# Hybrid encoder layer on one core: first-layer sums from GpSimd to VectorE, weight splits five products ahead, other load order in the drain and the mLSTM prelude

## Chip, core and metric

The kernel runs on one core of a Trainium2 chip, as one program. The metric is the device time of an execution in microseconds (us). TensorE (PE) does the matrix products, VectorE (DVE) and ScalarE (ACT) elementwise work, GpSimd (POOL) elementwise work and small steps, and SyncE (SP) only issues DMAs: its queue is in order, so a DMA that waits holds up those behind it.

## What is computed

```python
h = rms_norm(x, g_mix_norm)
z = h @ w_in                           # q, k, v, gate, i/f gates | latents, rotary key
y_a = mlstm_group(...)                 # bidirectional chunkwise mLSTM, 16 chunks of 128
y_b = mla_group(...)                   # 4 heads, softmax over all 2048 keys
x = x + concat(y_a, y_b) @ w_out       # out-projection, 1024 x 1024
h = rms_norm(x, g_ffn_norm)
x = x + square(relu(h @ w_ff1)) @ w_ff2  # 1024 -> 4096 -> 1024
```

x is 2048 x 1024, float32. Every product is done with both operands split into a high and a low part (`split`: ACT casts the high part at L48, DVE subtracts it at L49 to get the low part), as three matmuls per pair (L63 to L65).

## The kernel before

The projections at the start are placed by a scheduler and are the same in both kernels. All that follows is issued in an order written out by hand, engine by engine in program order:

- **Attention with mLSTM** (about 460 to 1160 us of the trace): 32 blocks of 256 queries, eight steps each. Each step issues scores (L1010 to L1014), their scaling by DVE with a running maximum (`p<-ps`, L1015), transposes of probabilities (`ptp`, L1045), their split (`pth`, `ptl`) and products with V (`pv`). A generator, advanced once a step, issues the mLSTM besides: first its gate arithmetic, called the prelude here (L556 to L660), then its chunks. In the prelude the decay table is stored (`d_dec`, L617) and loaded back as `decb` (L619). Each attention block also stores its inverse row sums (`d_rd`, L1031) and loads them back broadcast as `rb` (L1036), which scales the block's output `y` (L1062).
- **Drain** (1150 to 1190 us): the last blocks' products, while `OutProj.weights` loads the 4 MB of `w_out` in 256-KB halves into eight stage tiles (L1198) and splits them (`woh`, `wol`), one pair of halves a step; a half beyond the eighth takes the stage tile of a half just split. The tokens' tiles `y` and `x` go into a ring of eight tiles (`r`).
- **Out-projection** (1190 to 1376 us): 16 token tiles, `residual` (L1280), `normalise` (L1304) and `combine_x` (L1322), which forms sums of the normalised input for the first layer.
- **First feed-forward layer** (1376.75 to 2050 us): a two-level Strassen-like scheme. 32 passes `n` (16 groups of 256 columns for each half of the tokens) of seven products, twelve 128x512 matmuls each. For each product a 128x512 weight block, an original one or a sum of `w1_combine` (L1371), is split some products ahead (`w1_split`, tiles `r`, DVE `r L49`). Each product's PSUM result `pu` is added by DVE into accumulators `e` (L1470), and in four of the seven products ACT then does relu (L1473) and square (L1474). Sums of the results are formed by `u_combine` (L1507) and stored for the second layer. From n = 1 a generator `tokens` normalises and transposes the other half's eight token tiles between products (L1300 to L1322); from n = 14 `exchange` loads and splits that half's operands (L1404, L1405).
- **Second feed-forward layer** (2050 us to the end).

Of the kernel before, what the change touches and what calls it, by code (L numbers as in the profile page):

```python
# [18 lines left out]
P = 128  # L19
# [525 lines left out]
def mlstm_prelude(c, psM):  # L545
# [4 lines left out]
    with ExitStack() as st:  # L550
# [26 lines left out]
        nc.vector.reciprocal(wi, w)  # L577
        nc.vector.tensor_tensor(d, d, wi, op=ALU.mult)
        yield
        nc.vector.tensor_tensor(ln, ln, d, op=ALU.add)  # L580
        nc.vector.scalar_tensor_tensor(f, f, 0.0, ln, op0=ALU.min, op1=ALU.subtract)
        b, u, cu, gs = sb("b"), sb("u"), sb("cu"), sb("gs", (P, 2))
# [32 lines left out]
        nc.scalar.activation(it, M, AF.Exp, scale=-1.0, bias=mp)  # L615
        nc.scalar.activation(gd, gd, AF.Exp, scale=-1.0)
        nc.sync.dma_start(c.d_dec, dec)  # L617
        for par in range(2):
            nc.sync.dma_start(  # L619
                c.dec[par * 64:(par + 1) * 64],  # L620
                c.d_dec.rearrange("(a p c) o -> p o a c", p=2, c=NT)[par].to_broadcast((64, 4, NT)))
        yield
        x1, x2 = sb("x1", (P, 3, P)), sb("x2", (P, 2, P))
        p2 = bank()[:, 0:256].rearrange("p (a t) -> p a t", a=2)
# [6 lines left out]
            nc.tensor.transpose(p1[:, j, :], t, c.ident)  # L631
        yield
        nc.vector.tensor_copy(x1, p1)
        yield
        p4 = bank()[0:H, 0:256].rearrange("p (a t) -> p a t", a=2)
        for j in range(2):
# [32 lines left out]
def mlstm_steps(c, pool, ps, ld):  # L669
# [171 lines left out]

    kws, outs = {}, {}
    first = NT - 1
    for t in range(NT + 2):
        ch = first - t
        if ch >= 1:
            kws[ch] = weigh(1, NT - 1 - ch, ld[ch][1])
        if 1 <= ch + 1 <= first:
            v1 = ld.pop(ch + 1)[0]
            outs[ch + 1] = outer(kws.pop(ch + 1), v1)  # L850
        yield
        if 1 <= ch + 2 <= first:
# [3 lines left out]
        if t in (8, 10, 12, NT + 1):  # L856
            loads[{8: 0, 10: 1, 12: 2}.get(t, 3)](0)
        yield
    for d in range(2):
# [317 lines left out]
class OutProj:  # L1177
# [12 lines left out]
    def weights(self):  # L1190

        nc, c = self.c.nc, self.c
        raws = []

        def load(n):
            k, j = divmod(n, 2)
            raw = self.stage.tile([P, 512], F32, name="raw")
            nc.sync.dma_start(raw, c.w_out[k * P:(k + 1) * P, j * 512:(j + 1) * 512])  # L1198
            raws.append(raw)

        for n in range(8):
            load(n)
        yield
        self.yp = Ring(self.ent_ring(c.tc.tile_pool(name="ring", bufs=4, side="right", reuse_waits="tile")))
        self.wp = self.ent_w(c.tc.tile_pool(name="o_w", bufs=1, side="right", reuse_waits="tile"))
        yield
        for k in range(KD):
            if k in (1, 3):
                self.load_y(k // 2)
            elif k > 5:  # L1210
                self.load_x(k - 6)
            wh = self.wp.tile([P, D], F32R, name=f"woh{k}")
            wl = self.wp.tile([P, D], F32R, name=f"wol{k}")
            for j in range(2):
                cs = slice(j * 512, (j + 1) * 512)
                split(nc, wh[:, cs], wl[:, cs], raws.pop(0), eng=nc.gpsimd if j else None)
                if 2 * k + j + 8 < 2 * KD:
                    load(2 * k + j + 8)
            self.wo.append((wh, wl))
            yield  # L1220

# [96 lines left out]
def combine_x(c, b, t):  # L1318

    b11, b21, b12, b22 = b  # L1320
    for o, x, y in ((t[0], b12, b11), (t[1], b22, t[0]), (t[2], b22, b12), (t[3], b21, t[1])):
        c.nc.gpsimd.tensor_tensor(o, x, y, op=ALU.subtract)  # L1322


def store_x(c, g, i, b, t):
# [5 lines left out]
class FeedForward:  # L1331
# [35 lines left out]
    def w1_combine(self, n, name):  # L1367

        a, b, f = {"S1": ("A21", "A22", ALU.add), "S2": ("S1", "A11", ALU.subtract),
                   "S3": ("A11", "A21", ALU.subtract), "S4": ("A12", "S2", ALU.subtract)}[name]  # L1370
        self.c.nc.gpsimd.tensor_tensor(self.w1_part(n, name), self.w1_part(n, a), self.w1_part(n, b), op=f)  # L1371

    def w1_split(self, n, op):
        if (n, op) < (0, 2):
# [5 lines left out]
        self.w1[n, op] = wh, wl  # L1380

    def h_load(self, g, op, k):
        nc = self.c.nc
# [131 lines left out]
    def tokens(self):  # L1515

        c, nc = self.c, self.c.nc
        for i in range(4):
            b = []
            for q in range(2):  # L1520
                t = 8 + 4 * q + i
                for j in range(2):
                    x = self.stage.tile([P, 512], F32, name="raw")
                    nc.sync.dma_start(x, c.d_x1[t * P:(t + 1) * P, j * 512:(j + 1) * 512])
                    b.append(x)
            junk = self.stage.tile([P, 512], F32, name="raw")
# [11 lines left out]
            combine_x(c, b, tt)  # L1538
            for _ in range(4):
                yield  # L1540
            store_x(c, 1, i, b, tt)
            for _ in range(4):
                yield

    def layer1(self, extra):
        N = 2 * self.NU
        prev = None
        for n in range(N):
            g, f = divmod(n, self.NU)
            if n == 1:  # L1550
                extra = self.tokens()
            elif n == self.NU - 2:
                for _ in extra:
                    pass
                extra = self.exchange()
            for p in range(7):
                self.product(n, p)
                m, q = divmod(7 * n + p + 3, 7)
                if m < N:
                    self.w1_split(m, q)  # L1560
                self.flush()
                if n > 0:
                    if p == 1:
                        self.u_combine(n - 1, "S1")
                        self.u_combine(n - 1, "S2")
                    elif p == 2:
                        self.u_combine(n - 1, "S3")
                    elif p == 3:
                        self.u_combine(n - 1, "S4")
                if prev:  # L1570
                    self.evacuate(*prev)
                prev = n, p, self.ps
                if p == 0:
                    self.w1_combine(n, "S4")
                elif p == 1 and n + 1 < N:
                    self.w1_combine(n + 1, "S1")
                    self.w1_combine(n + 1, "S2")
                elif p == 3:
                    if n + 2 < N:
                        self.load_w1(n + 2)  # L1580
                    if n + 1 < N:
                        self.w1_combine(n + 1, "S3")
# [151 lines left out]
def out_and_ffn(c):  # L1734
    tc = c.tc
    with ExitStack() as s_stage:
        with ExitStack() as s_e:
# [10 lines left out]
            with ExitStack() as s_y:  # L1748
# [14 lines left out]
                for s in range(NT - 2):  # L1763
# [10 lines left out]
                    if s < 8:  # L1774
                        o.normalise(s)
                    if s % 2 == 0 and 2 <= s <= 8:
                        combine_x(c, *pair)
# [9 lines left out]
                    if s == 12:  # L1787
                        ff.load_w1(0)
                        ff.load_w1(1)
                    elif s == 13:  # L1790
                        for name in ("S1", "S2", "S3"):
                            ff.w1_combine(0, name)
                        ff.w1_split(0, 0)
# [3 lines left out]
                ff.w1_split(0, 1)  # L1797
                for _ in range(3):
                    pieces_on(4)
                for i in range(2):  # L1800
                    o.residual(NT - 2 + i, po[i])
            with ExitStack() as s_ps:
                ff.open1(s_f1.enter_context, s_ps.enter_context)
                ff.w1_split(0, 2)
                prev = ff.layer1(ff.h_pieces(0, pieces))
                s_f1.close()
                s_h1.close()
# [45 lines left out]
```

## Time and profile before

| | |
|---|---|
| median of 3 runs | 2668.52 us (2662.75 to 2672.58) |
| profiled execution | 2668.72 us, span 2666.9 us |
| PE busy | 2594.1 us, 97% |
| VectorE busy | 1615.9 us, 61% |
| ScalarE busy | 1193.9 us, 45% |
| GpSimd busy | 826.3 us, 31% |

The span is from the first to the last recorded instruction; the 1.8 us between it and the execution's time are start and end. Times in the rows are from the span's start. An engine's busy share is over the whole span, so it says little of a single stage.

### The profile page before, as it was taken

How to read it: one execution, taken by the hardware profiler on the slowest of the kernel's cores; microseconds unless marked ns; L12 is line 12 of the kernel's file. 1: busy time of each engine (PE TensorE's matmuls, PEld its weight loads, DVE VectorE, ACT ScalarE, POOL GpSimd, SP SyncE). 2: the span in 40 equal slices, each digit the busy share in tenths (PEclk: the TensorE clock that was granted, in tenths of full speed). 3: DMA queues.
4: the chain of work that ended last, by engine and by line, in shares of the span. 5: the costliest groups of instructions: out<-in, count | busy, mean ns of one | idle time of the engine just before them, and what ended most of it. 6: DMA issues, size and time to landing. Idle time of an engine off the chain costs nothing. (4 is left out here: it accounts for less than half of the span.)

```text
span 2666.9 us, 37134 instructions
## 1 busy us (share of the span) xinstructions
PE 2594.1 (97%) x13227; PEld 2180.9 (82%) x13227; DVE 1615.9 (61%) x2914; ACT 1193.9 (45%) x2457; POOL 826.3 (31%) x730
## 2 busy tenths in 40 slices
PE   8999999899999999989999999989999999999999
PEld 6888887788888888878887777668887888888887
DVE  5585475666666666654356666666666477666443
ACT  6455443446656566542134444544444333332332
POOL 1211210123224232212116666555655133233000
PEclk9999999999999999999999999999999999999999
DMA  4344244245464565446664555834445844444552
GB/s 154 122 131 153 95 134 135 70 118 125 92 117 108 92 115 101 68 127 190 210 208 137 169 196 170 256 135 141 146 154 173 316 150 142 143 143 153 206 174 103
DMA packets 298870, 391.58 MB, mean 147 GB/s; under 512 B 33281, under 2 KB 187196, under 8 KB 298684
## 3 DMA queue, kind: packets, MB, share of 16 engines
q1 hardware_dynamic: 296380, 385.01, 49.0%
q10 hardware_dynamic: 2304, 4.20, 0.4%
q8 instruction: 104, 1.70, 0.3%
q14 instruction: 82, 0.67, 0.1%
HBM read 256.94 MB, written 132.17 MB: 146 GB/s over the span
## 5 line engine op out<-in xcount | busy, mean ns | idle before, releaser
L63 PE MATMUL pd<-w2h,uh 128*128 128x512 f32 x896 | 349.3, 390 | 1.3 <-ACT w2h L48 1.3
L64 PE MATMUL pd<-w2l,uh 128*128 128x512 f32 x896 | 349.4, 390 | 0.4 <-DVE w2l L49 0.4
L65 PE MATMUL pd<-w2h,ul 128*128 128x512 f32 x896 | 349.3, 390 | 0.0
L49 DVE TENSOR_TENSOR ul<-ur,uh 128x1024 fp32r<-128x1024 f32 x110 | 146.9, 1336 | 253.7 <-ACT uh L48 253.5
L49 DVE TENSOR_TENSOR ptl<-ptp,pth 128x512 fp32r<-128x512 f32 x256 | 176.7, 690 | 193.8 <-ACT pth L48 193.7
L48 ACT CAST uh<-ur 128x1024 fp32r<-128x1024 f32 x110 | 116.0, 1054 | 396.3 <-PE pd L64 378.4
L49 DVE TENSOR_TENSOR r<-w1raw,r 128x512 fp32r<-128x512 f32 x160 | 187.6, 1173 | 140.8 <-ACT r L48 140.8
L48 ACT CAST pth<-ptp 128x512 fp32r<-128x512 f32 x256 | 149.2, 583 | 253.7 <-PE ptp L1045 252.3
L1473 ACT ACTIVATE e<-e 128x512 f32<-128x512 f32 x128 | 80.9, 632 | 346.8 <-DVE e L1470 346.8
L1507 POOL TENSOR_TENSOR e<-e 128x512 f32<-128x512 f32 x128 | 183.4, 1443 | 120.8 <-ACT e L1474 118.2
L1015 DVE TENSOR_SCALAR_CACHE_REDUCE p<-ps 128x512 f32<-128x512 f32 x256 | 175.1, 684 | 45.4 <-PE ps L1014 44.1
L63 PEld LDWEIGHTS pd<-w2h,uh 128*128 128x128 f32 x896 | 168.6, 188 | 36.8 <-ACT w2h L48 1.8
L64 PEld LDWEIGHTS pd<-w2l,uh 128*128 128x128 f32 x896 | 168.6, 188 | 36.1 <-DVE w2l L49 1.1
L65 PEld LDWEIGHTS pd<-w2h,ul 128*128 128x128 f32 x896 | 168.5, 188 | 35.0
L63 PE MATMUL pv<-pth,vh 128*128 128x256 f32 x512 | 146.3, 286 | 15.1 <-DVE y L1062 7.7
L1629 POOL TENSOR_TENSOR r<-wr,r 128x512 f32<-128x512 f32 x48 | 87.0, 1813 | 223.3 <-DMA wr<-in_w 141.0
L1045 PE MATMUL ptp<-ident,p 128*128 128x128 f32 x1024 | 154.2, 274 | 0.0
L63 PE MATMUL pz<-wh,hh 128*128 128x512 f32 (+1 forms) x384 | 150.3, 393 | 3.1 <-ACT hh L48 3.1
L65 PE MATMUL pz<-wh,hl 128*128 128x512 f32 (+1 forms) x384 | 150.7, 393 | 0.0
L1470 DVE TENSOR_TENSOR e<-pu,e 128x512 f32<-128x512 f32 x224 | 149.6, 680 | 1.4 <-POOL e L1507 1.2
L64 PE MATMUL pz<-wl,hh 128*128 128x512 f32 (+1 forms) x384 | 150.3, 391 | 0.0
L64 PE MATMUL pv<-ptl,vh 128*128 128x256 f32 x512 | 146.2, 285 | 1.1 <-DVE ptl L49 0.9
(392 smaller groups left out, 6832.4 us busy)
## 6 DMA issues: line engine op xcount, KB each, us to landing
d_u<-e SPq DMA_DIRECT2D x224, 256.0 KB
ur<-d_u SPq DMA_DIRECT2D x110, 512.0 KB
w1raw<-in_w SPq DMA_DIRECT2D x64, 512.0 KB
wr<-in_w SPq DMA_DIRECT2D x96, 256.0 KB
raw<-in_w_in SPq DMA_DIRECT2D x48, 256.0 KB
xt<-in_x SPq DMA_DIRECT2D x16, 512.0 KB
mb<-d_M SPq DMA_DIRECT2D x32, 256.0 KB
r<-in_x SPq DMA_DIRECT2D x16, 512.0 KB
```

The source lines that it names most:

```text
L48: nc.scalar.copy(hi, src)
L49: (eng or nc.vector).tensor_tensor(lo, src, hi.bitcast(F32), op=ALU.subtract)
L63: nc.tensor.matmul(out, ah, bh, start=first, stop=False)
L64: nc.tensor.matmul(out, ah, bl, start=False, stop=False)
L65: nc.tensor.matmul(out, al, bh, start=False, stop=last)
L1015: nc.vector.tensor_scalar(probs[b, a][:, j, :], o, SCALE, None, op0=ALU.mult, op1=ALU.max, accum_out=maxes[b, a][:, j:j + 1])
L1045: nc.tensor.transpose(pt[:, k, :], p[:, j, k * P:(k + 1) * P], c.ident)
L1470: nc.vector.tensor_tensor(out, o, t, op=ALU.add)
L1473: nc.scalar.activation(t, t, AF.Relu)
L1507: self.c.nc.gpsimd.tensor_tensor(o, a, b, op=f)
L1629: nc.gpsimd.tensor_tensor(R, wr, R, op=ALU.subtract)
```

## The change

- **Sums.** `combine_x`, `w1_combine` and `u_combine` are issued on VectorE and no longer on GpSimd: 16 sums in the out-projection, and in the first layer 16 of `combine_x`, 128 of `w1_combine` and 128 of `u_combine`. They are issued one per step, behind the step's evacuation. `u_combine` has its four at products 1 to 4 (before: 1, 1, 2, 3).
- **Splits.** A generator `weights1` issues the first layer's splits, sums and loads in their order. From n = 1 to n = 12 it is five products ahead, elsewhere three (before: three everywhere); it takes up to two splits in a step until it is there. The split tiles alternate between both halves of the ring (eight tiles) up to n = 12.
- **Drain.** The rows of w_out for k = 4 to 7 are loaded at once, as four 512-KB transfers into four ring tiles, ahead of the first split; the `y` and `x` loads stand a step or more elsewhere.
- **mLSTM prelude.** One more step stands between the exchange of the gates and their sums (L580 to L583). The two `decb` loads are issued three steps later. The backward chunk loop has one step less.

```diff
@@ mLSTM prelude
         nc.vector.tensor_tensor(d, d, wi, op=ALU.mult)
         yield
+        yield
         nc.vector.tensor_tensor(ln, ln, d, op=ALU.add)
@@
         nc.sync.dma_start(c.d_dec, dec)
-        for par in range(2):
-            nc.sync.dma_start(
-                c.dec[par * 64:(par + 1) * 64],
-                c.d_dec.rearrange("(a p c) o -> p o a c", p=2, c=NT)[par].to_broadcast((64, 4, NT)))
         yield
...
         nc.vector.tensor_copy(x1, p1)
+        for par in range(2):
+            nc.sync.dma_start(
+                c.dec[par * 64:(par + 1) * 64],
+                c.d_dec.rearrange("(a p c) o -> p o a c", p=2, c=NT)[par].to_broadcast((64, 4, NT)))
@@
-    for t in range(NT + 2):
+    for t in range(NT + 1):
@@ OutProj.weights
         self.wp = self.ent_w(c.tc.tile_pool(name="o_w", bufs=1, side="right", reuse_waits="tile"))
+        for k in range(4, KD):
+            if k == 6:
+                self.load_y(0)
+                yield
+            raw = self.yp.tile([P, D], F32)
+            nc.sync.dma_start(raw, c.w_out[k * P:(k + 1) * P, :])
+            raws += [raw[:, 0:512], raw[:, 512:]]
         yield
         for k in range(KD):
...
                 split(nc, wh[:, cs], wl[:, cs], raws.pop(0), eng=nc.gpsimd if j else None)
-                if 2 * k + j + 8 < 2 * KD:
-                    load(2 * k + j + 8)
@@ combine_x, w1_combine, u_combine
-        c.nc.gpsimd.tensor_tensor(o, x, y, op=ALU.subtract)
+        c.nc.vector.tensor_tensor(o, x, y, op=ALU.subtract)
+        yield
...
-        self.c.nc.gpsimd.tensor_tensor(o, a, b, op=f)
+        self.c.nc.vector.tensor_tensor(o, a, b, op=f)
@@ layer1
                 self.product(n, p)
-                m, q = divmod(7 * n + p + 3, 7)
-                if m < N:
-                    self.w1_split(m, q)
+                ahead = 7 * n + p + 1 + (5 if 0 < n < self.NU - 3 else 3)
+                todo = min(2, ahead - self.nsplit)
+                for i in range(todo):
+                    next(self.wsteps, None)
+                    if i + 1 < todo:
+                        next(self.wsteps, None)
                 self.flush()
...
                 prev = n, p, self.ps
...
+                if todo > 0:
+                    next(self.wsteps, None)
+                if n > 0 and 1 <= p <= 4:
+                    self.u_combine(n - 1, f"S{p}")
                 next(extra, None)
```

SP in the prelude, behind the first store of an inverse row sum that stands there (`d_rd`; `dec` tiles are the decay table, `raw<-d_kn` and `d_kr` the keys of the next head). Before:

```order
L1031 DMA d_rd<-rd_5115 128x2x1
L617 DMA d_dec<-dec 128x1
L619 DMA decb<-d_dec 64x4x16 x2
L1036 DMA rb<-d_rd 128x256
L953 DMA raw<-d_kn 128x512
L956 DMA raw<-d_kr 64x512 x2
L1031 DMA d_rd<-rd_5267 128x2x1
```

and now:

```order
L1032 DMA d_rd<-rd_5115 128x2x1
L1037 DMA rb<-d_rd 128x256
L618 DMA d_dec<-dec 128x1
L954 DMA raw<-d_kn 128x512
L957 DMA raw<-d_kr 64x512 x2
L632 DMA decb<-d_dec 64x4x16 x2
L1032 DMA d_rd<-rd_5255 128x2x1
```

The load of `rb` moved ahead of the table's store and load; the table's load moved behind the keys.

SP in the drain, behind the last mLSTM store (`d_ya`; `r` are ring tiles, the loads of `in_w_out` the out-projection's weights). Before:

```order
L838 DMA d_ya<-sgt 128x512
L1198 DMA raw<-in_w_out 128x512 x2
L1235 DMA r_13345<-d_ya 128x512
L1236 DMA r_13345<-d_yb 128x4x128
L1198 DMA raw<-in_w_out 128x512 x2
L1031 DMA d_rd<-rd_13179 128x2x1
L1198 DMA raw<-in_w_out 128x512 x2
L1065 DMA d_yb<-y 128x256
L1235 DMA r_13401<-d_ya 128x512
L1236 DMA r_13401<-d_yb 128x4x128
L1198 DMA raw<-in_w_out 128x512 x2
L1036 DMA rb<-d_rd 128x256
```

and now:

```order
L839 DMA d_ya<-sgt 128x512
L1212 DMA r_13307<-in_w_out 128x1024
L1212 DMA r_13309<-in_w_out 128x1024
L1240 DMA r_13311<-d_ya 128x512
L1241 DMA r_13311<-d_yb 128x4x128
L1212 DMA r_13333<-in_w_out 128x1024
L1212 DMA r_13335<-in_w_out 128x1024
L1032 DMA d_rd<-rd_13182 128x2x1
L1240 DMA r_13373<-d_ya 128x512
L1241 DMA r_13373<-d_yb 128x4x128
L1066 DMA d_yb<-y 128x256
L1037 DMA rb<-d_rd 128x256
```

All weights stand ahead of `d_rd` now; between the last `d_yb` and `rb` two loads of `in_x` are left out of the second fence.

DVE in the first layer, in a pass without token work (`r` split tiles, `w1raw` loaded weights, `sw` weight sums). Before:

```order
L49 TENSOR_TENSOR r_16132<-w1raw_15939,r_16132 128x512
L1470 TENSOR_TENSOR e<-pu,e 128x512
L49 TENSOR_TENSOR r_16151<-sw,r_16151 128x512
L1470 TENSOR_TENSOR e<-pu,e 128x512 x2
L49 TENSOR_TENSOR r_16178<-w1raw_15941,r_16178 128x512
L1470 TENSOR_TENSOR e<-pu,e 128x512
```

and now:

```order
L49 TENSOR_TENSOR r_16241<-w1raw_16061,r_16241 128x512
L1500 TENSOR_TENSOR e<-pu,e 128x512
L1377 TENSOR_TENSOR w1raw_16061<-w1raw_16061 128x4x128
L1537 TENSOR_TENSOR e<-e 128x512
L49 TENSOR_TENSOR r_16270<-sw,r_16270 128x512
L1500 TENSOR_TENSOR e<-pu,e 128x512
L1537 TENSOR_TENSOR e<-e 128x512
L49 TENSOR_TENSOR r_16291<-w1raw_16063,r_16291 128x512
L1500 TENSOR_TENSOR e<-pu,e 128x512
L1377 TENSOR_TENSOR w1raw_16063<-w1raw_16063,sw 128x4x128
L1537 TENSOR_TENSOR e<-e 128x512
```

One or two sums (L1377, L1537) now stand behind an addition of a product's result (L1500), where before the next split stood.

## Rows read from the trace of the kernel before

**Rows 1.** Windows: length, busy us of PE, PEld, DVE, ACT, POOL, PEclk, DMA share, GB/s.
```profile
462.00:523.00 61.00, 49.50 (x266) 41.16 (x265) 36.76 (x103) 27.34 (x40) 12.54 (x16) 0.94 0.22 61
523.00:1150.00 627.00, 624.41 (x4246) 555.94 (x4245) 406.27 (x1059) 370.97 (x812) 175.83 (x184) 1.00 0.53 105
1150.00:1190.00 40.00, 29.00 (x181) 25.54 (x180) 23.84 (x52) 24.48 (x50) 12.55 (x10) 0.87 0.57 142
1190.00:1376.00 186.00, 186.00 (x881) 155.12 (x880) 78.42 (x114) 40.72 (x87) 34.50 (x43) 1.00 0.66 207
1396.08:1678.12 282.04, 267.81 (x1157) 214.95 (x1156) 177.82 (x214) 129.69 (x240) 181.35 (x144) 0.98 0.52 169
1678.12:1759.02 80.90, 67.19 (x253) 49.38 (x252) 57.37 (x62) 41.67 (x66) 39.97 (x25) 0.94 0.66 217
1759.02:2010.27 251.25, 251.25 (x1093) 205.24 (x1092) 161.96 (x180) 118.28 (x207) 152.50 (x104) 1.00 0.43 144
```

**Rows 2.** Waits of PE, 462 to 523: total, times, longest (us).
```profile
PE pv L63 <- DVE y L1062: 5.6, 1, 5.6
PE ps L1010 <- DVE p L1015: 4.1, 1, 4.1
```

**Rows 3.** Timeline of DVE, 475 to 517: start, us, instruction, [idle before <-releaser].
```profile
477.15 0.58 DVE L580 TENSOR_TENSOR ln<-ln,d 128x128 f32<-128x128 f32 x1 [1.61 <-ACT ln L574]
...
480.44 0.66 DVE L1015 TENSOR_SCALAR_CACHE_REDUCE p<-ps 128x512 f32<-128x512 f32 x1
...
516.00 0.42 DVE L1062 TENSOR_TENSOR y<-pv,rb 128x256 f32<-128x256 f32 x1 [6.43 <-DMA rb<-d_rd]
```

**Rows 4.** Timeline of SP's DMA issues, 487 to 508.
```profile
487.93 0.37 SPq L1031 DMA_DIRECT2D d_rd<-rd  x1
496.10 0.34 SPq L617 DMA_DIRECT2D d_dec<-dec  x1
505.28 1.27 SPq L619 DMA_DIRECT2D decb<-d_dec  x2
506.65 0.55 SPq L1036 DMA_DIRECT2D rb<-d_rd  x1
```

**Rows 5.** Timeline of ACT in the drain.
```profile
1182.38 1.27 ACT L48 CAST woh<-raw 128x512 fp32r<-128x512 f32 x2 [2.50 <-DMA raw<-in_w_out]
1183.55 0.58 ACT L48 CAST pth<-ptp 128x512 fp32r<-128x512 f32 x1
```

**Rows 6.** Timeline of SP's DMA issues in the drain.
```profile
1167.14 0.38 SPq L1031 DMA_DIRECT2D d_rd<-rd  x1
...
1177.17 0.33 SPq L1036 DMA_DIRECT2D rb<-d_rd  x1
```

**Rows 7.** Timeline of PE at the end of the drain.
```profile
1184.18 0.58 PE L63 MATMUL pv<-pth,vh 128*128 128x256 f32 x1 [6.22 <-ACT pth L48]
...
1188.78 0.48 PE L63 MATMUL po<-woh,r 128*128 128x512 f32 x1
```

**Rows 8.** Timeline of all engines, 969 to 976: a load of `rb` and its use.
```profile
969.31 0.33 SPq L1036 DMA_DIRECT2D rb<-d_rd  x1
...
974.93 0.41 DVE L1062 TENSOR_TENSOR y<-pv,rb 128x256 f32<-128x256 f32 x1
```

**Rows 9.** Waits of VectorE, 1396 to 1759.
```profile
DVE r L49 <- ACT r L48: 82.9, 50, 1.9
DVE raw L1304 <- POOL nr L59: 25.2, 8, 4.2
```

**Rows 10.** Timeline of DVE in pass 24 of the first layer.
```profile
1899.76 0.69 DVE L49 TENSOR_TENSOR r<-w1raw,r 128x512 fp32r<-128x512 f32 x1 [1.87 <-ACT r L48]
1900.37 0.68 DVE L1470 TENSOR_TENSOR e<-pu,e 128x512 f32<-128x512 f32 x1
1902.92 1.38 DVE L49 TENSOR_TENSOR r<-sw,r 128x512 fp32r<-128x512 f32 x1 [1.87 <-ACT r L48]
...
1919.27 0.69 DVE L49 TENSOR_TENSOR r<-w1raw,r 128x512 fp32r<-128x512 f32 x1 [1.87 <-ACT r L48]
```

More of the change, by code (lines that the diff above doesn't have):

```diff
@@ L855, in mlstm_steps @@
             ld[ch - 3] = mlstm_v(c, ch - 3), mlstm_k(c, ch - 3)
-        if t in (8, 10, 12, NT + 1):
+        if t in (8, 10, 12, NT):
             loads[{8: 0, 10: 1, 12: 2}.get(t, 3)](0)
@@ L1199, in load @@
             raws.append(raw)
-        for n in range(8):
+        for n in range(KD):
             load(n)
@@ L1205, in weights @@
         self.wp = self.ent_w(c.tc.tile_pool(name="o_w", bufs=1, side="right", reuse_waits="tile"))
+        for k in range(4, KD):
[5 more added lines that the diff above has]
+            raws += [raw[:, 0:512], raw[:, 512:]]
         yield
         for k in range(KD):
[L1208 to L1213, printed above, removed]
+            if k == 1:
+                self.load_y(1)
+            elif k in (3, 4):
+                self.load_x(k - 3)
+            wh, wl = (self.wp.tile([P, D], F32R, name=f"wo{part}{k}") for part in "hl")
             for j in range(2):
@@ L1370, in w1_combine @@
                    "S3": ("A11", "A21", ALU.subtract), "S4": ("A12", "S2", ALU.subtract)}[name]
-        self.c.nc.gpsimd.tensor_tensor(self.w1_part(n, name), self.w1_part(n, a), self.w1_part(n, b), op=f)
+        self.c.nc.vector.tensor_tensor(self.w1_part(n, name), self.w1_part(n, a), self.w1_part(n, b), op=f)
     def w1_split(self, n, op):
-        if (n, op) < (0, 2):
+        if n < self.NU - 3:
             w = self.ring.tile([P, 2, 4, P], F32R)
@@ L1380, in w1_split, with weights1 @@
         self.w1[n, op] = wh, wl
+    def weights1(self):
+        N = 2 * self.NU
+        self.nsplit = 0
+        self.w1_combine(0, "S1")
+        self.w1_combine(0, "S2")
+        for n in range(N):
+            for q in range(7):
+                self.w1_split(n, q)
+                self.nsplit += 1
+                yield
+                if q == 0:
+                    self.w1_combine(n, "S3")
+                elif q == 2:
+                    self.w1_combine(n, "S4")
+                elif q == 5 and n + 1 < N:
+                    self.w1_combine(n + 1, "S1")
+                elif q == 6:
+                    if n + 2 < N:
+                        self.load_w1(n + 2)
+                    if n + 1 < N:
+                        self.w1_combine(n + 1, "S2")
+                yield
     def h_load(self, g, op, k):
@@ L1537, in tokens @@
             tt.append(junk)
-            combine_x(c, b, tt)
-            for _ in range(4):
-                yield
+            yield from combine_x(c, b, tt)
             store_x(c, 1, i, b, tt)
@@ L1557, in layer1 @@
                 self.product(n, p)
-                m, q = divmod(7 * n + p + 3, 7)
-                if m < N:
-                    self.w1_split(m, q)
-                self.flush()
[L1562 to L1569, printed above, removed]
+                ahead = 7 * n + p + 1 + (5 if 0 < n < self.NU - 3 else 3)
[4 more added lines that the diff above has]
+                        next(self.wsteps, None)
+                self.flush()
                 if prev:
@@ L1572, in layer1 @@
                 prev = n, p, self.ps
[L1573 to L1582, printed above, removed]
+                if todo > 0:
+                    next(self.wsteps, None)
+                if n > 0 and 1 <= p <= 4:
+                    self.u_combine(n - 1, f"S{p}")
                 next(extra, None)
@@ L1776, in out_and_ffn @@
                     if s % 2 == 0 and 2 <= s <= 8:
-                        combine_x(c, *pair)
+                        for _ in combine_x(c, *pair):
+                            pass
                     o.load_x(s + 2)
@@ L1790, in out_and_ffn @@
                     elif s == 13:
-                        for name in ("S1", "S2", "S3"):
-                            ff.w1_combine(0, name)
-                        ff.w1_split(0, 0)
+                        ff.wsteps = ff.weights1()
+                        next(ff.wsteps)
                 po = o.project(NT - 2, NT - 1)
@@ L1796, in out_and_ffn @@
                 ff.open_h1(s_h1.enter_context)
-                ff.w1_split(0, 1)
+                next(ff.wsteps)
+                next(ff.wsteps)
                 for _ in range(3):
@@ L1803, in out_and_ffn @@
                 ff.open1(s_f1.enter_context, s_ps.enter_context)
-                ff.w1_split(0, 2)
+                for _ in range(3):
+                    next(ff.wsteps)
                 prev = ff.layer1(ff.h_pieces(0, pieces))
```

## The prediction

> **What bounds the kernel now.** I read PE's share first: it is busy 97% of the span (the table above), so apart from fewer matmuls only some 73 us of idle PE can be won, and what it loses to a lower clock. The windows by stage tell where that is [rows 1]: 11.5 us in the prelude (462 to 523), 2.6 in the 627 us of attention behind it, 11.0 in the drain, nothing in the out-projection and nothing in passes 17 to 29 of the first layer, where 13 passes take 251.25 us, 19.33 each. At that pace passes 1 to 13 would take 251.3 and took 282.04; passes 14 to 16 would take 58.0 and took 80.90. So 30.7 and 22.9 us lie there, and the change touches just these places.
>
> What bounds passes 1 to 16 is not seen in PE's row but in VectorE's waits [rows 9]: it waits for ACT (82.9 us) and for GpSimd's small steps (25.2 us), never for PE. DVE and ACT are one chain, late throughout, and PE waits for its split weights. The timeline shows a link [rows 10]: DVE splits (1899.76), adds a product's result 0.61 later, then stands 1.87 us while ACT does relu, square and the next cast; the next split starts 3.16 us after the first. The reader is to see two things: this idle time, four times a pass, and that the subtraction of 0.69 us becomes 1.38 in the next row, which I read as GpSimd's sums beside it. Four such steps, two of split and addition (1.22) and one of a split alone (0.61) are 15.7 us; the same row of the next pass comes 19.51 later (1919.27). The 3.8 us between I take for that contention. With 19.51 against PE's 19.33, the chain is as slow as PE even without the tokens' work.
>
> **First layer.** Taken from GpSimd and added on DVE: eight 128x512 sums a pass. No row shows such a sum on DVE; the nearest is the addition, pitch 0.61 (1899.76 to 1900.37); the other end is 1.38, a subtraction beside GpSimd. I take 0.61, since GpSimd then has no sums. In the order now shown the sums stand behind the addition, so in a relu step up to two (1.22) hide in the 1.87 us of idle; in the other steps they lengthen the chain. Five products ahead, products 1, 2 and 4 are the others, with two sums each: 15.7 + 6 x 0.61 = 19.3 a pass. Three ahead it is five sums: 18.7.
> Passes 1 to 12: (19.3 - 19.5) x 12 = -2. Two more splits taken at n = 1: 2 x 0.61, +1.3. Pass 13 leaves two out and is three ahead after them: -0.8 - 1.3 = -2. Passes 14 to 16, three ahead: -0.8 x 3 = -2.5. `combine_x` adds 16 sums on DVE, half of them hidden: +4.9, against contention of as many sums now, which I take as 5.5: -0.6. Pass 0 ends with the chain less late, since its sums no longer run beside the splits of h: -2, an estimate. Together about **-8**. The 25.2 us of waits in the normalisation stay, as its small steps remain on GpSimd.
> The lead of five products I cost at nothing in itself. It lets PE run on while the chain catches up; where the chain is late on average, it only moves the wait. Two products more are 2 x 2.76 = 5.5 us of PE once, and n = 13 falls back to three. Without lateness on average it would be worth much; that is the first rival.
> In passes 17 to 31, PE is full at 19.33 and the chain at 18.7 is now the faster: no change.
> Bounds: with the six unhidden sums at 1.38 a pass is 24.0, +54 in passes 1 to 12; as GpSimd is no partner any more I go a good third of that way, to +20. The other end is the first rival's -47. The out-projection's 16 sums lie under a PE that is full for 186 us with DVE busy 78 [rows 1]: nothing; without that cover, 16 x 0.61 = 10.
>
> **Prelude.** Two stalls. At 516.00 DVE waits 6.43 us for `rb` and PE 5.6 behind it [rows 2, 3]. `rb` was issued at 506.65 because it stood behind `decb`, which waited from 496.10 to 505.28 for the store of `d_dec` [rows 4]. Now `rb` stands right behind its own store, `d_rd`, of 487.93; the nearest price of that wait is the drain's, 1167.14 to 1177.17, 10.0 us [rows 6]. So it is issued at about 498, lands as long after as now (516.0 - 506.7 = 9.4) at 507.3, and is wanted at 509.6: 2.3 us to spare, all 5.6 gone. Queued behind the waiting `rb` are `d_dec` (two us later) and the keys of the next head; behind `decb`, which may wait until 507, only the next `d_rd` at about 509. With the stall goes a clock dip: the granted clock was 0.94 over 61 us, 3.7 us of full-speed work lost behind two stalls; half is 1.8.
> At 477.15 DVE had stood 1.61 us for ACT, then did 3.29 us of gate arithmetic before the scaling at 480.44 for which PE waited 4.1 [rows 2, 3]. One step later, two scalings stand ahead of it and hide the 1.61, but the 3.29 stay in front of a scaling: of 4.1 I leave 2.9, -1.2. Of the stage's other 1.8 us of idle PE I take 1.1 as gone: a product of the running maximum (`mr`) now has products with V ahead of it. Sum 5.6 + 1.8 + 1.2 + 1.1 = **-9.7**; from -6 (the store of `d_rd` 4 us slower, or the gate stall unchanged) to -13, all idle of the stage and the clock.
>
> **Attention behind it.** PE is idle 2.6 of 627 us. The chunk steps fall beside other steps of a block, and one is less at the end: **-1**, between -2.6 and +3 (three new waits of a us).
>
> **Drain.** PE's longest wait, 6.2 us, is for `pth` [rows 7], and ACT's order shows why: at 1182.38 it has stood for the last weights, and the cast of `pth` is queued behind them at 1183.55 [rows 5]. Those weights could be issued only when a stage tile came free. Now they are issued before the `d_rd` of 1167.14, and 2 MB with one `y` tile (2.5 MB) at the 207 GB/s of the stage behind [rows 1] take 12 us: there by 1179. The last block's output then waits for `rb`, issued at 1177.17 [rows 6]. How long that takes is between 5.6 us (the shortest use behind an issue, [rows 8]) and the 9.4 of the prelude: its output at 1182.8 to 1186.6, and the projection, now at 1188.78 [rows 7], one us later at 1184 to 1187.6. I take 1184.8, near the short end, as DMA is by then done with the weights: **-4**. The lower end is -1; the upper -9, if `rb` and the store of `d_rd` both gain from the earlier loads. What speaks for a loss of a few us: `d_rd` now stands behind all the weights in SP's queue.
>
> **Sum.** -8 - 9.7 - 1 - 4 = -22.7; the profiled execution took 2668.72 us, 1.8 more than its span, and lies 0.2 above the median. So **2646 us**.
>
> **Rivals.**
> (a) The stalls of the first layer are bursts, not lateness on average, and five products of lead take them up; that PE runs full from n = 17 on with the same chain at 19.51 speaks for it. Then about 24 of 30.7 (the rest is token transposes) and 22.9 go: -47 there, 2668.7 - 47 - 14.7 = 2607. Against it speaks that DVE never waits for PE.
> (b) VectorE becomes the bound. The sums of a relu step don't fit behind the addition, since ACT's cast runs ahead or the sum is what the next split waits for; all eight then lengthen the chain: 15.7 + 4.9 = 20.6 a pass. This decides from where a pass is over 19.33, so passes 17 to 31 suffer as well, 15 x 1.3 = +19, and passes 1 to 16 16 x 1.1 = +18: 2668.7 - 14.7 + 37 = 2691. The busy time is against it: 161.96 of 251 us now, and 13 x 4.9 = 64 more leaves a tenth free.
> The Trainium skill has a rule for this ("Perfetto Trace Analysis", Optimizing Scalar/DVE Operations): where DVE is saturated, handing work to ScalarE or even GpSimd may make sense, which is this edit backwards; it adds that DVE and GpSimd share a port, so that moving work between the two may not help. By it the time is that of this rival; the 1.38 beside the 0.69 us agrees with its second half only.
> (c) The change does little of what it says: the drain stays bound by DMA (-1), `rb` is as late behind its own store (-4), and the first layer's chain gains nothing (0): 2663.
>
> **Numbers.** What counts as no change here is 0.5%, 13 us. The forecast has 0.58 (2633 to 2657), (a) 0.18, (b) 0.08, (c) 0.16. The 8 in 10 leave out the far half of (a) and (b): 2609 to 2667. Faster takes most of the forecast (0.55), (a) and a little of (c): 0.76; same the rest of these and a mild (b): 0.17; slower 0.07.
>
> **What would show it.** In the profile after: no wait for `rb` near 510, and a gate stall of about 3 us; the out-projection's first product near 1174 (9.7 + 1 + 4 earlier); DVE's `r L49` all at 0.69; DVE's waits for ACT in passes 1 to 16 smaller, those for `nr` about the same 25 us; passes 14 to 16 still over 70 us in all. Wrong it would be if passes 1 to 13 come near 19.33 each plus the token transposes (then the lead matters), or if passes 17 to 31 rise above 19.33.

## The result, and the profile after

The changed kernel took 2648.62 us in the median of five runs (2643.21 to 2653.41) against 2668.52 before: a ratio of 0.9925, 95% interval 0.9904 to 0.9946. Run again beside later experiments it was 2647.44 against 2663.6, 0.9944 (0.9931 to 0.9957). The forecast was 2646. The sum came out; the terms did not all, and errors of opposite sign met in it, as will be seen.

The windows of the changed kernel answer to [rows 1]; the last three are passes 1 to 13, 14 to 16 and 17 to 29, at the places where they now lie (busy us of PE, PEld, DVE, ACT, POOL, then PEclk, DMA share, GB/s):

```profile
462.00:523.00 61.00, 56.95 (x330) 47.83 (x329) 43.99 (x115) 31.47 (x46) 13.18 (x17) 0.97 0.35 63
523.00:1150.00 627.00, 619.19 (x4187) 550.85 (x4186) 398.88 (x1051) 371.80 (x806) 175.20 (x184) 1.00 0.51 105
1150.00:1190.00 40.00, 32.63 (x195) 27.84 (x195) 23.34 (x47) 23.95 (x49) 12.82 (x10) 0.91 0.59 155
1190.00:1376.00 186.00, 186.00 (x882) 155.07 (x881) 84.86 (x139) 43.34 (x93) 7.90 (x24) 1.00 0.66 207
1391.78:1662.80 271.02, 262.43 (x1157) 213.48 (x1156) 196.42 (x325) 127.80 (x236) 9.70 (x24) 0.99 0.53 172
1662.80:1740.91 78.11, 65.46 (x254) 46.29 (x252) 60.29 (x89) 41.11 (x66) 0.00 (x0) 0.98 0.69 235
1740.91:1992.18 251.27, 251.27 (x1093) 205.32 (x1092) 180.44 (x290) 123.77 (x212) 0.00 (x0) 1.00 0.44 151
```

The prelude lost 7.5 us of idle PE, but the long attention stage, which had 2.6 us of it, has 7.8 now. Passes 1 to 13 are 11.0 us shorter, 14 to 16 are 2.8 shorter, and 17 to 29 are what they were.

A reader who wants to know where time went sets the same instruction of both traces side by side. These are the starts of the same matmul on PE in the two profiled executions (us; blocks and passes counted from 0):

| matmul | before | after | lead |
|---|---|---|---|
| first score of block 1 | 475.78 | 475.84 | +0.1 |
| first score of block 3 | 526.03 | 516.84 | -9.2 |
| first score of block 7 | 611.87 | 611.73 | -0.1 |
| first score of block 31 | 1140.34 | 1139.32 | -1.0 |
| first of the out-projection | 1188.78 | 1183.02 | -5.8 |
| 65th of the out-projection | 1203.91 | 1199.61 | -4.3 |
| first of pass 1 | 1396.08 | 1391.78 | -4.3 |
| first of pass 14 | 1678.12 | 1662.80 | -15.3 |
| first of pass 17 | 1759.02 | 1740.91 | -18.1 |
| 337th of the second layer | 2129.26 | 2109.48 | -19.8 |

The prelude won 9.2 us, as forecast, and nine were lost again within 95 us. So the out-projection's first product starts at 1183.02, not near 1174 as the prediction has it. The waits of PE in that stage show the place (total, times, longest):

```profile
PE pm L694 <- issue: 6.2, 12, 2.1
PE pm L802 <- POOL iz L775: 0.9, 1, 0.9
```

`pm<-v,kw` (L694) is the product of the backward mLSTM scan. The trace names no releaser ("issue"), but the timeline of all engines at its longest wait does:

```profile
561.91 1.07 ACT L48 CAST pth<-ptp 128x512 fp32r<-128x512 f32 x2 [5.39 <-PE ptp L1046]
562.53 0.69 DVE L49 TENSOR_TENSOR ptl<-ptp,pth 128x512 fp32r<-128x512 f32 x1 [3.56 <-ACT pth L48]
563.14 0.60 DVE L706 SCALAR_TENSOR_TENSOR C<-C,decb,pm 128x129 f32<-128x129 f32 x2
563.84 0.66 PE L694 MATMUL pm<-v,kw 128*64 128x129 f32 x8 [2.15 <-issue]
```

The product of one scan step writes the bank `pm` that VectorE's update of the step before (L706) reads, and starts just as that update ends. The update is queued behind the split of the probabilities, which waits for ACT's cast. PE also drops in granted clock behind this wait (0.5 for 3.4 us from 564.9). In the trace before, the same pair has a microsecond between the update's end (555.27) and the product:

```profile
554.67 0.60 DVE L705 SCALAR_TENSOR_TENSOR C<-C,decb,pm 128x129 f32<-128x129 f32 x2
556.31 0.66 PE L693 MATMUL pm<-v,kw 128*64 128x129 f32 x8
```

In the first layer the waits of VectorE over passes 1 to 16 answer to [rows 9]:

```profile
DVE r L49 <- ACT r L48: 58.8, 46, 1.9
DVE raw L1309 <- POOL nr L59: 19.0, 7, 4.0
```

and its timeline shows the sums where the change put them:

```profile
1457.30 0.69 DVE L49 TENSOR_TENSOR r<-w1raw,r 128x512 fp32r<-128x512 f32 x1 [1.87 <-ACT r L48]
1457.91 0.68 DVE L1500 TENSOR_TENSOR e<-pu,e 128x512 f32<-128x512 f32 x1
1458.51 0.68 DVE L1377 TENSOR_TENSOR sw<-w1raw,w1raw 128x512 f32<-128x512 f32 x1
1460.46 0.69 DVE L49 TENSOR_TENSOR r<-w1raw,r 128x512 fp32r<-128x512 f32 x1 [1.27 <-ACT r L48]
```

The sum (L1377) has a pitch of 0.6 us, the next split still starts 3.16 us behind the first, and the idle time of 1.87 us has become 1.27: the sum is hidden. The splits of passes 1 to 16 are at 0.69 us, all 111 that the trace has.

### The profile page after: what moved, and what is told of

Its sections match the earlier page's. It is cut to its first block, busy times and chain, and to the rows that moved or that the text cites. A ratio compares the mean times of both kernels' runs of the same rounds, so it can differ in the third digit from the quotient of the medians.

```text
span 2647.7 us, 37081 instructions
## 1 busy us (share of the span) xinstructions
PE 2587.3 (98%) x13227; PEld 2176.5 (82%) x13227; DVE 1660.6 (63%) x3202; ACT 1201.9 (45%) x2457; POOL 404.8 (15%) x442
## 5 line engine op out<-in xcount | busy, mean ns | idle before, releaser
L49 DVE TENSOR_TENSOR r<-w1raw,r 128x512 fp32r<-128x512 f32 x160 | 110.5, 690 | 103.7 <-ACT r L48 102.5
L1500 DVE TENSOR_TENSOR e<-pu,e 128x512 f32<-128x512 f32 x224 | 150.7, 685 | 3.2 <-PE pu L65 3.2
L65 PE MATMUL pv<-pth,vl 128*128 128x256 f32 x512 | 145.3, 284 | 0.0
```

What stands on the lines that cost most here:

```text
L49: (eng or nc.vector).tensor_tensor(lo, src, hi.bitcast(F32), op=ALU.subtract)
L65: nc.tensor.matmul(out, al, bh, start=False, stop=last)
L1500: nc.vector.tensor_tensor(out, o, t, op=ALU.add)
```

## Experiments

Kernels of one set ran on the same chip and share the runs of the kernel before; ratios are to it, with 95% intervals.

**The table's load alone** (e_table). The kernel before with this edit:

```diff
         nc.sync.dma_start(c.d_dec, dec)
-        for par in range(2):
-            nc.sync.dma_start(
-                c.dec[par * 64:(par + 1) * 64],
-                c.d_dec.rearrange("(a p c) o -> p o a c", p=2, c=NT)[par].to_broadcast((64, 4, NT)))
         yield
...
         nc.vector.tensor_copy(x1, p1)
+        for par in range(2):
+            nc.sync.dma_start(
+                c.dec[par * 64:(par + 1) * 64],
+                c.d_dec.rearrange("(a p c) o -> p o a c", p=2, c=NT)[par].to_broadcast((64, 4, NT)))
```

> The kernel before with one edit: the table's load (decb) three steps later; no step added, the backward loop as before. Theory 'step': the 8.5 us that the changed kernel gives back between 526 and 612 us come from the added step, which puts the backward scan's products (pm<-v,kw) into the other kind of step. Then here the wait for rb at 516 goes (5.6 us and its clock dip, -7), the scores lead by 6.5 to 7.5 us at 526 and still by 6 or more at 612, and the whole is 2661 to 2663. Rival 'table': the scan is late because the table and the loads queued behind it on SP come later. Then the lead at 526 is the same, and is down to 0 to 1.5 us at 612; the whole 2667 to 2669.

Measured: the wait for `rb` is gone, the scores gain 6.4 us between blocks 1 and 3 and keep it to block 7 (leads of +1.7, -4.65, -4.67). So the later load alone costs the scan nothing. The whole was 2662.6 against 2664.54, a ratio of 0.9991 (0.9982 to 1.0001): within the forecast of 2661 to 2663, but less than this trace won against the profile before. The drain's experiment below shows that the wait which this edit removes is not always as long as in that profile.

**An empty step ahead of the scan** (e_parity). The changed kernel with:

```diff
     kws, outs = {}, {}
     first = NT - 1
+    yield
```

> The changed kernel with one more empty step ahead of the backward scan, so that its products fall into the steps that they had before the change. Theory 'step': the 12 waits of pm<-v,kw (6.2 us) and the clock dip at 565 go, the lead of 9 us at 526 is still 8 at 612; the forward chunks behind it stand as before the change, which costs about 1; in all -6 to -8 against the changed kernel, 2641 to 2643. Rival 'table': the waits stay, and the whole is within 1 of the changed kernel's 2648.6 or longer.

Measured: the waits of PE in that stage are again those of the kernel before:

```profile
PE pm L694 <- issue: 1.4, 5, 0.4
PE pm L694 <- POOL kw L687: 0.6, 1, 0.6
```

The lead at block 3 (-7.3, from +0.5 at block 1) is the same at block 7, and -7.8 at block 31. Theory "step" holds in the trace. The ratio was 0.9921 (0.9906 to 0.9936), 2644.09 us, a microsecond over the range expected. Its interval overlaps those of the changed kernel (0.9925 and 0.9944), so the scan's share is read from the traces.

**Sums and lead, each alone.** The changed kernel with the sums on GpSimd (e_gpsums):

```diff
-        c.nc.vector.tensor_tensor(o, x, y, op=ALU.subtract)
+        c.nc.gpsimd.tensor_tensor(o, x, y, op=ALU.subtract)
... (the same in w1_combine and u_combine)
```

> The changed kernel with the three kinds of sums issued on GpSimd again, at the same places; lead of five kept. Theory 'chain': the lead moves waits but doesn't shorten the chain of VectorE and ScalarE; with subtractions at 1.2 to 1.8 us again a pass of the chain is back at 19.5 and more, so passes 1 to 16 take 358 to 366 us (before 362.9, changed 349.1), and at passes 17 on the lag of the additions behind the products grows again. Rival 'lead': five products ahead is what took up the stalls. Then passes 1 to 16 take 347 to 353 us here as well.

and the changed kernel with a lead of three (e_lead3):

```diff
-                ahead = 7 * n + p + 1 + (5 if 0 < n < self.NU - 3 else 3)
+                ahead = 7 * n + p + 1 + 3
```

> The changed kernel with a lead of three products everywhere; sums on VectorE kept. Theory 'chain': a pass with three ahead costs 18.7 against 19.3 us of chain, the two extra splits at n = 1 are not needed, and the lead is given back at n = 13 anyway: passes 1 to 16 take 340 to 350 us, no longer than the changed kernel's 349.1. Rival 'lead': without the two products more the stalls at the tokens come back, and passes 1 to 16 take 355 to 362 us.

Measured, passes 1 to 13 and 14 to 16, first for GpSimd's sums, then for the lead of three:

```profile
1392.43:1668.24 275.81, 264.51 (x1158) 214.01 (x1157) 173.39 (x210) 127.85 (x237) 179.66 (x142) 0.98 0.53 170
1668.24:1749.05 80.81, 65.75 (x253) 47.23 (x252) 56.81 (x63) 42.16 (x67) 41.17 (x27) 0.96 0.68 226
```

```profile
1390.77:1657.61 266.84, 262.45 (x1157) 210.29 (x1156) 197.93 (x328) 126.97 (x236) 10.12 (x24) 1.00 0.55 179
1657.61:1735.26 77.65, 65.69 (x253) 47.67 (x252) 59.26 (x87) 41.94 (x66) 0.00 (x0) 0.95 0.64 221
```

Passes 1 to 16 took, in us:

| | three ahead | five ahead |
|---|---|---|
| sums on GpSimd | 362.9 (before) | 356.6 |
| sums on VectorE | 344.5 | 349.1 (after) |

Two of the four steps between these cells change one thing. In the right column only the engine of the sums differs: VectorE's are worth 7.5 us. In the lower row only the lead differs: five products cost 4.6. Later profiles agree on the lead: 350.2 and 350.4 with five (e_again, e_parity), 344.7 with three (e_step_lead). The two steps from the kernel before, 6.3 along the upper row and 18.4 down the left column, also have the sums at new places in the order and the split tiles over both halves of the ring, and no run separates these.

The first expectation missed on both sides: 356.6 is neither the 358 to 366 of "chain" nor the 347 to 353 of "lead". Its last part missed as well: the lag of the results behind the products (defined below) stays between 2.3 and 3.4 us from pass 18 to the end, where in the kernel before it grows by 0.18 a pass. The second held for "chain". Ratios: 0.9965 (0.9952 to 0.9978) and 0.9922 (0.9907 to 0.9937); the second is not apart from the changed kernel's within the intervals.

**The drain alone** (e_drain). The kernel before with the change's `OutProj.weights` and nothing else.

```diff
+        for k in range(4, KD):
+            if k == 6:
+                self.load_y(0)
+                yield
+            raw = self.yp.tile([P, D], F32)
+            nc.sync.dma_start(raw, c.w_out[k * P:(k + 1) * P, :])
...
-                if 2 * k + j + 8 < 2 * KD:
-                    load(2 * k + j + 8)
```

> The kernel before with the drain's edit alone. Prediction's step: the projection begins 4 us earlier than before against the scores of the last block, bounded by rb (7 at most); the wait of PE for pth (6.2) goes, a wait for y takes part of its place; the whole 2663 to 2665 where before is 2668.5, a ratio of 0.998 to 0.999. Rival (c): the drain stays bound by its loads, the wait for pth is still over 4 us, and the whole is within 1 us of before.

Measured: the projection begins 4.0 us earlier against block 31's scores, PE's wait for `pth` is down to 0.9 at most, and one for `y` of 4.6 has come, as forecast:

```profile
PE ypt L1256 <- DVE y L1062: 4.6, 1, 4.6
PE pv L63 <- DVE y L1062: 2.1, 1, 2.1
PE pv L63 <- ACT pth L48: 1.6, 4, 0.9
```

By the 65th product of the out-projection only 1.7 of the 4.0 us are left; PE's granted clock is low there (0.5 for 6.8 us from 1178.4). The whole is 2664.02 against 2663.6, 1.0006 (0.9996 to 1.0015), where 0.998 to 0.999 was expected: no gain that the runs can tell, so of rival (c) the time came true and the wait did not. The drain of the kernel before varies too: from the last score to the projection it took 30.5 us in the profile before and 28.8 in e_table's, with a wait for `pth` of 6.2 and 4.6. This profile holds a second finding, in the prelude that it shares with the kernel before:

```profile
513.35 0.42 DVE L1062 TENSOR_TENSOR y<-pv,rb 128x256 f32<-128x256 f32 x1 [3.09 <-DMA rb<-d_rd]
513.92 0.36 PE L63 MATMUL pv<-pth,vh 128*128 128x256 f32 x1 [2.29 <-DVE y L1062]
```

The stall for `rb`, 5.6 us in the profile before [rows 2], was 2.3 here, with the same code and no clock dip behind it. So what the prelude's edit is worth can differ between executions by some 3 us and the clock dip.

**The two losses taken out, and the changed kernel beside them.** e_again is the changed kernel; e_step_lead has the empty step and the lead of three.

> The changed kernel itself, as the partner of the others of this set on the same chip. Both theories: 0.9925 of the kernel before, within its interval, and the same stages as in its first profile to a microsecond or two (passes 1 to 16 near 349, the scan's 12 waits of pm<-v,kw).

> The changed kernel with the empty step ahead of the backward scan and a lead of three products everywhere. If the two losses found are of different places and causes, they add: about 7 us less at 612 (scores lead by 8) and 4 to 5 less in passes 1 to 16 (344 to 346): 10 to 12 us under the changed kernel of this set, near 2637. If what is won ahead of the drain is waited out there, at the load of rb behind the store of d_rd, 5 to 8.

Measured: 2647.44 and 2638.78 us, 0.9944 (0.9931 to 0.9957) and 0.9907 (0.9893 to 0.9920), 8.7 us apart: between the two expectations, and clear of the intervals. The two profiled executions are 4.8 apart. There the scan and passes 1 to 16 give 5.8 and 5.5 us, while e_again was 2 us earlier at block 1, won 2 more in the prelude, and its drain kept 4.1 us where this one kept 1.1.

The profile of e_again corrects the first one in a point. The scan's product waits 13 times in it, 4.8 us in all, none over 0.43 and with no clock dip, and from block 3 to block 7 it loses 5.8 us, not nine. It is the same in e_gpsums and e_lead3, which have the same scan. The wait of 2.1 us and the dip behind it belong to one execution; the 12 or 13 short waits come with the step.

**The tokens' scaling one product later** (e_norm_later). The same, and in `tokens`:

```diff
-                normalise(c, self.sp, x, x, [junk, junk])
-                for _ in range(4):
+                r = normalise(c, self.sp, x, x, [junk, junk], later=True)
+                yield
+                for j in range(2):
+                    nc.vector.tensor_scalar(x[j], x[j], r, None, op0=ALU.mult)
+                for _ in range(3):
                     yield
```

> The same as the run with step and lead, and the tokens' scaling by VectorE one product later than its squares, so that VectorE does not stand while ScalarE squares and GpSimd takes the root. Theory 'chain': the waits of VectorE for nr (19 us in the changed kernel) go, passes 1 to 13 come from 267 down to 258 to 260 (13 x 19.33 and the transposes), and since the chain arrives less late at the exchange, passes 14 to 16 lose some us too: 10 to 16 us less than the run with step and lead, near 2625. Rival 'PE order': PE waits for the transposed tokens as such, and a scaling one product later is one more product of waiting there: passes 1 to 13 stay at 265 or more.

```profile
1383.82:1642.22 258.40, 258.40 (x1157) 211.81 (x1156) 197.80 (x328) 126.99 (x236) 12.64 (x24) 1.00 0.56 185
1642.22:1719.85 77.63, 65.25 (x254) 47.42 (x253) 59.25 (x87) 41.94 (x66) 0.00 (x0) 0.96 0.65 222
```

Passes 1 to 13 are at their floor, PE busy throughout; 14 to 16 gained nothing (77.65 in e_step_lead), against the expectation. 2628.35 us, 0.9867 (0.9853 to 0.9880), 10.4 less than e_step_lead, where 10 to 16 was expected.

**The lead again, without those waits** (e_norm_lead5): the last kernel with the change's lead of five.

> The run with the tokens' later scaling, with the changed kernel's lead of five in passes 1 to 12. Theory 'chain': without the normalisation waits a pass costs the chain 19.3 us with five ahead and 18.7 with three, both not over PE's 19.33 plus transposes, so passes 1 to 13 take 258 to 260 with either, and the lead is worth nothing; at most 2 us more, from the chain reaching the exchange later. Rival: the lead itself costs 4 us or more, as it did beside the waits (349.1 against 344.5 for passes 1 to 16).

```profile
1385.31:1648.12 262.81, 260.33 (x1157) 213.12 (x1156) 198.10 (x328) 128.01 (x236) 12.44 (x24) 0.99 0.55 180
1648.12:1725.43 77.31, 64.87 (x254) 47.38 (x253) 58.93 (x86) 41.95 (x66) 0.00 (x0) 0.96 0.68 231
```

My theory missed, the rival held: 4.4 us more in passes 1 to 13. The whole was 2635.53, 0.9883 (0.9867 to 0.9900); its interval overlaps that of e_norm_later, so the cost rests on the windows. PE's waits name the place:

```profile
PE dpt L1321 <- DVE raw L1567: 2.5, 2, 2.1
```

These are 2.5 of the 4.4 us; most of the rest is PE at a granted clock of 0.5 for 3.4 us behind the longer of the two (its busy time is 260.33 us, not 258.40). PE's order has a token's transposes a fixed number of products behind its scaling. With five products ahead the other work of VectorE and ScalarE is later (ACT's copy of product 0 in pass 8 starts 9.4 us behind its matmuls instead of 5.2), and PE reaches the transposes first. That the two splits more on VectorE are what makes it later is my reading of the order. The same wait stands in the changed kernel, whose waits for splits are the shorter ones:

```profile
PE dpt L1318 <- DVE raw L1309: 8.4, 3, 3.7
PE pu L65 <- DVE r L49: 3.5, 6, 0.6
```

In e_lead3 there is none for `dpt`, and 7.8 us for the splits:

```profile
PE pu L65 <- DVE r L49: 7.8, 9, 1.5
```

**The order of the drain's loads**, three kernels on top of e_norm_later: the last half of the weights behind `d_rd` (e_rd_first), `in_x` behind `rb` (e_x_late), both (e_rd_x). `whole(k)` is the load of a whole row block, as in the change.

```diff
             if k == 1:
+                whole(6)
+                whole(7)
                 self.load_y(1)
-            elif k in (3, 4):
-                self.load_x(k - 3)
+            elif k in (6, 7):
+                self.load_x(k - 6)
```

> The run with the tokens' later scaling, with the loads of w_out for k = 6 and 7 issued behind the last d_rd, no longer ahead of it. Theory 'rb floor': what bounds the end of the drain is the last rb, which waits for the store of d_rd, and that store is slow because four 512-KB loads are queued ahead of it (12 to 13 us from d_rd to rb against 10.0 in the kernel before). Then d_rd to rb takes 10 us or less here, PE's wait for y behind the last block goes from 4.6 to 2 or less, and the projection begins 2 to 3 us earlier; if the clock dip behind that wait goes too, up to 2 more. Rival 'weights': the last weights are then late again, and PE waits for pth behind their casts; the projection begins no earlier.

> The run with the tokens' later scaling, with the two 512-KB loads of in_x issued behind the last rb, as in the kernel before. Theory 'queue': the last rb lands late (4.2 us behind its issue there, 7 to 9 behind it where d_rd came first) because 1 MB of in_x, needed only a projection later, is in flight ahead of it; without that d_rd to rb is 10 us or less, PE's wait for y goes from 3.4 to 1.5 or less and the projection begins 2 to 4 us earlier against the scores of the last block. Rival 'latency': store and load of 128 KB cost some 17 us together whatever is beside them; the wait stays at 3 us or more.

> Both edits of the drain: the last half of w_out behind d_rd, and in_x behind rb. Theory 'queue': nothing large is ahead of d_rd or rb but 1 MB of w_out; the pair takes 13 us or less, y no longer waits for rb, and the projection is bounded by the last pv, 3 to 5 us earlier than in the run with the later scaling; in all up to 4 us less than there. Rival 'latency': no earlier than in the run with d_rd first alone. Rival 'weights': PE waits for pth behind the casts of the last weights instead.

From the issue of the last `d_rd` to the issue of `rb`, and from there to VectorE's `y`, in us:

| | d_rd to rb | rb to y | sum | PE waits for y |
|---|---|---|---|---|
| e_norm_later | 12.7 | 4.6 | 17.3 | 3.35 |
| e_rd_first | 8.5 | 8.7 | 17.2 | 3.32 |
| e_x_late | 11.7 | 5.7 | 17.5 | 3.50 |
| e_rd_x | 9.6 | 7.6 | 17.2 | 3.56 |

In e_rd_first the first leg came down to under 10 us, as "rb floor" had it, and the second grew by as much. The sum doesn't move: "queue" and "rb floor" fell, "latency" held in its outcome. Why the pair ends after 17 us in these four is not settled. It is no fixed time: in the changed kernel, e_again, e_gpsums and e_lead3 it is 15.2 to 15.6. In e_rd_x `y` was no longer recorded as waiting for `rb`. The ratios, 0.9862 (0.9848 to 0.9877), 0.9863 (0.9846 to 0.9879) and 0.9849 (0.9834 to 0.9864), are those of e_norm_later within their intervals. All four of these kernels took less time than both kernels of this study, clear of the intervals; e_norm_later took 19.1 us less than the changed kernel of its set.

## Why the prediction was right in its sum, and where its steps failed

Both profiles of the changed kernel, against the one profile before:

| term | forecast | first profile | e_again |
|---|---|---|---|
| ahead of block 1 | 0 | +0.1 | -1.5 |
| prelude | -9.7 | -9.3 | -9.8 |
| attention behind it | -1 | +8.2 | +5.0 |
| drain, to the 65th product behind it | -4 | -3.3 | -4.1 |
| first layer, passes 1 to 16 | -8 | -13.8 | -12.8 |
| from there to the 337th of the second layer | 0 | -1.7 | +0.2 |
| sum | -22.7 | -19.8 | -22.9 |

That the first profile's sum came within 3 us of the forecast is in part luck: attention lost 9.2 us against its term, and the first layer won 5.8 more than its own.

**Attention.** The step "the chunk steps fall beside other steps of a block, and one is less at the end: -1" failed. I looked at the idle time there was (2.6 us) and bounded the loss by three new waits of a microsecond. What I did not follow was the added empty step through the backward scan: it moves all its steps by one, and a score step with products of V ahead of the scan's product is exchanged for one without. In the trace before, VectorE's update ended about a microsecond ahead of the product that needs its bank; that slack became 12 or 13 waits, and in the first profile one of them was long, with a clock dip behind it. That the added step is the cause e_parity shows: one step more, and the waits are those of before.

**Prelude.** Right in the trace by its mechanism: `rb` was issued at 494.01 and no wait is left; the gate stall was 2.5 us with another wait of 0.9, where 2.9 were left. But its largest part, 5.6 and a dip of 1.8, is what one execution of the kernel before showed. In e_drain's execution of the same code it was 2.3. A sum worked out against one profile counts such a wait in full.

**Drain.** Right in the trace: the wait for `pth` went and one for `y` took its place; 30.5 us from the last score to the projection became 25.6 (26.1 to 27.5 in the other runs with this drain). I called `rb` the bound. It is where VectorE stands for it ahead of `y`, 1.5 to 3.3 us in seven of these profiles; in the changed kernel's first one it stood 0.1 us, behind other work, in e_gpsums 0.5, and in e_again, e_lead3 and e_rd_x it was not recorded as waiting. The clock dip behind the new wait, which I had not priced, took 1.5 of 4.7 us back in the first profile, 2.3 of 4.0 in e_drain and nothing in e_again. In e_drain's times nothing of the term is seen.

**First layer.** The pace was right: from pass 17 the results' lag behind the products falls by 0.65 us a pass, so the chain runs at 19.33 - 0.65 = 18.7, as worked out for three ahead. Before, it grew by 0.18 a pass there, which is the 19.51 of the prediction. Mis-sized were three terms. With the lag at product 0 of a pass (the start of ACT's copy behind the end of the product's last matmul) the 13.8 us come apart. In pass 1, before and after:

```profile
1398.65 0.40 PE L65 MATMUL pu<-h0h,r 128*128 128x512 f32 x1
1405.03 0.58 ACT L1477 COPY e<-pu 128x512 f32<-128x512 f32 x1
```

```profile
1394.35 0.40 PE L65 MATMUL pu<-h0h,r 128*128 128x512 f32 x1
1396.99 0.58 ACT L1507 COPY e<-pu 128x512 f32<-128x512 f32 x1
```

The lag was 6.0, 7.6 and 4.3 us in passes 1, 13 and 17 before, and 2.2, 10.2 and 5.1 after. The head start, "-2, an estimate", is 6.0 - 2.2 = 3.7. The chain of passes 1 to 12, PE's time and the growth of the lag, went from 262.1 + 1.6 to 250.9 + 7.9: -4.9 where -1.3 was forecast (-2 + 1.3 - 0.6), 3.6 us more. Most likely the tokens' share of the contention is more than the 5.5 us that I set for it; no run separates it. PE runs 10.2 - 7.6 = 2.6 us further ahead at pass 13, and 1.9 of it is given back by pass 17. Passes 13 to 16 of the chain came out at -4.4 (-4.5 forecast). The lead, forecast as nothing in itself, costs: 4.6 us more than three products in the first pair of profiles. The pace worked out for five ahead (19.3 against 18.7) gave the sign, but not the waits for the tokens' transposes.
Rival (a), bursts, may have a part of the truth that the sum gave none: with GpSimd's sums and five ahead passes 1 to 16 are 6.3 us shorter than before, all of it in pass 2 (27.4 to 21.0), with the new places as a second possible cause. Rival (b), VectorE as the bound, did not come: it is busy 180 of 251 us in passes 17 to 29, and PE is full there.

That VectorE never waits for PE, only for ACT and GpSimd, was the right thing to read: with the waits for `nr` removed, passes 1 to 13 came from 267.1 us in e_step_lead to 258.4.

## What to carry to other kernels

When one empty step goes into a hand-written order, follow every later step of that generator to what now stands beside it; slack of a microsecond is invisible in a list of waits. Before a lead is raised, look for work at a fixed place in another engine's order that will now come later; here that cost more than the lead gave. The lagging chain of two engines was shortened by taking contention and waits out of it. And a term taken from one profiled wait on a DMA should be checked in a second execution before it is counted in full.

## What was not expected of the hardware

- A store of a small table and its load back (`d_rd`, `rb`) took 15.2 to 17.5 us from the first issue to the use in the twelve profiles with the changed drain, with the two legs between 7.9 + 7.3 and 13.0 + 4.5. Large loads stand beside them in all of these, and no run has the pair alone.
- VectorE's subtraction in the first layer took 1.18 us on average in the profile before and 1.10 in e_gpsums, where GpSimd's sums run beside it, and 0.69 with the sums on VectorE. The addition of a product's result, which has one input in PSUM, stayed under 0.70 in all 224 cases of each of these profiles. The Trainium skill ("SBUF — State Buffer", Who interferes with whom) has it that a VectorE instruction with two inputs in SBUF contends with a GpSimd instruction that reads SBUF, and one with at most one such input does not. The trace agrees in both halves; what the subtraction lost on average was 0.4 to 0.5 us.
